# First q products of a decoder step: shift and scale in parts of 256, 256 and 512 features instead of two of 512, and cache loads issued right behind adaLN

## The chip, the cores and the metric

The kernel runs on one core of a Trainium2 chip. The metric is the device time of one execution in microseconds (us). Three executions of the kernel before the change took 1012.66, 1013.51 and 1015.45 us; the median is 1013.51 us. The profile shown below comes from one further execution, of 1013.97 us, whose records span 1012.2 us from the first to the last instruction.

## The reference

One layer of a decoder trunk for two groups of tokens that share the weights: a prompt of 512 tokens and 8 sample tokens, each sample token with 1024 cached tokens in pages of 128. The width is 1024, there are 16 heads of 64, and all data are float32.

```
m = adaLN(c) -> (shift1, scale1, gate1, shift2, scale2, gate2)   # silu(c) @ ada_w + ada_b
h = RMSNorm(x) * (1 + scale1) + shift1
z = h @ w_in  -> rg_x | rg_gate | q | k | v | forget logits | merge gate A | merge gate B
branch A: causal conv -> RG-LRU -> * gelu(rg_gate) -> @ w_proj_a
branch B: forgetting attention over q, k, v, log f -> @ w_proj_b
x = x + gate1 * ((sigmoid(gA) * A + sigmoid(gB) * B) @ w_o)
x = x + gate2 * SwiGLU(RMSNorm(x) * (1 + scale2) + shift2)
y = RMSNorm(x)
```

The sample tokens attend to cached keys and values, and to the running sum of a cached log forget value (`cache_logf`), all of which are gathered by a page table.

## The kernel before

**Tiling.** The activations lie transposed: eight tiles of 128 features by 520 tokens (512 prompt, 8 sample). Each matmul product takes 128 weight columns by half of the tokens (260), and is done with float32 values split in two parts: weights into `whi` and `wlo`, activations `h` into `hh` and `hl`. Each 128-feature step of a product is three matmuls (hi by hi, lo by hi, hi by lo). ACT casts the high part (`whi`, `hh`), DVE subtracts it for the low part (`wlo`, `hl`). A full product (128 output columns, all 8 feature tiles, both token halves) is 48 matmuls.

**The start.** SP issues, in this order, the parameters, the eight `x` tiles, the weights of adaLN for features 0 to 511 of shift1 and scale1 (`araw`, eight loads of 512 KB, one for each 128 rows of `ada_w`), a small constant load (`cs`: the identity), the first weights of q (`wraw`), and then adaLN's weights for features 512 to 1023. `first_mod` multiplies a loaded `araw` tile with silu(c): four matmuls of 256 columns side by side, written to four groups of 32 rows of one bank (`adaf`). `keep_busy` puts matmuls behind them whose results nobody reads (`idle`). `first_mod_end` copies the bank (`adas`, ACT), transposes it (`adaft`, PE), adds the biases (`mod`, DVE) and makes the amplitude (`n1amp`, DVE). Meanwhile ACT squares `x`, DVE adds the squares in two groups of four, PE sums them over the features with a matrix of ones (`ss`), and ACT and DVE take the root and the reciprocal over 128 by 520 (`r`). `norm_x` multiplies `x` by `r` (`xn`). `first_h(f)` makes `hh` and `hl` of one feature tile: ACT for the prompt tokens of `hh`, POOL for the eight sample columns of `hr` (two small operations), ACT for the cast of these eight, DVE for `hr` and `hl`.

**q.** Output columns are six tiles q0 to q5 here (q6 and q7 come later as ordinary products). q's products over features 0 to 511 run first (`qp` in the records: q0 to q2, then q3 to q5), with adaLN's second half between them, and are copied to `qpart`. Then q0 to q5 run over features 512 to 1023 (`q` in the records) and are added to `qpart` (`qadd`).

**What follows.** A numbered list of units (`chunks`, `units`) sets the order of the later products xr, gr, ga, gb, k, v and so on. A table (`KEYS`) says how many cached key pages are loaded with each unit, and DVE sums the pages in between (`key_sum`). Instructions are queued on each engine in a fixed order, and each engine works its queue in that order; `issue_after` fixes such an order between two instructions of different steps. A tile taken from a pool waits for the readers of the tile that had its buffer: `pg` has 7 buffers (adaLN's weights, key and value pages), `wraw` has 2 (product weights, and the cached log f `lfp`), `whi` and `wlo` have 3 each. A load that SP issues also waits until the load eight places ahead of it on SP has landed.

The cached log f (`past_load`) is one indirect load, issued by POOL once the page list `idx` has landed; `past_turn` transposes it (`lft`, PE) and sums it on POOL. In the kernel before, `past_load` comes with q4 and `past_turn` with q5, and the first key pages are loaded by POOL with q4.

## Time and profile before

| | |
|---|---|
| three executions | 1012.66, 1013.51, 1015.45 us |
| profiled execution | 1013.97 us, span of its records 1012.2 us |
| mean granted TensorE clock | 0.998 |
| PE busy | 990.4 us, 98% of the span |
| DVE, ACT, POOL busy | 791.0, 564.7, 342.8 us |
| DMA | 206.12 MB, mean 204 GB/s |
| first q product starts | 23.71 us |

PE is the engine that is busy nearly throughout. "Busy" counts the modelled length of an instruction; matmuls overlap, so the start of one to the start of the next is what a matmul takes of PE's time. In a timeline row stand the start, the time from the start of the first to the end of the last of the merged instructions, the engine, the line, the operation, what it writes and reads, the count, and in brackets how long the engine had been idle before and what released it. A float32 matmul that isn't split shows as two records (an `x8` row of `adaf` is four matmuls).

### The profile page before, as it was taken

How to read it: one execution, taken by the hardware profiler on the slowest of the kernel's cores; microseconds unless marked ns; L12 is line 12 of the kernel's file. 1: busy time of each engine (PE TensorE's matmuls, PEld its weight loads, DVE VectorE, ACT ScalarE, POOL GpSimd, SP SyncE). 2: the span in 40 equal slices, each digit the busy share in tenths (PEclk: the TensorE clock that was granted, in tenths of full speed). 3: DMA queues.
4: the chain of work that ended last, by engine and by line, in shares of the span. 5: the costliest groups of instructions: out<-in, count | busy, mean ns of one | idle time of the engine just before them, and what ended most of it. 6: DMA issues, size and time to landing. Idle time of an engine off the chain costs nothing.

```text
span 1012.2 us, 21376 instructions
## 1 busy us (share of the span) xinstructions
PE 990.4 (98%) x8020; PEld 913.6 (90%) x8020; DVE 791.0 (78%) x1400; ACT 564.7 (56%) x1161; POOL 342.8 (34%) x440
## 2 busy tenths in 40 slices
PE   5999999999999999999999999999999999999996
PEld 2899999999898988888888878999999999999996
DVE  5678899989999887887655454869888888779864
ACT  4524679866952477777783233554444444445453
POOL 1136121323243244654400001483342442434212
PEclk9999999999999999999999999999999999999999
DMA  9799856889879998997767995333334243233122
GB/s 335 262 315 288 242 170 190 264 261 298 277 234 354 326 308 267 321 276 239 254 204 264 332 337 161 85 94 96 97 92 126 63 126 97 71 106 105 63 64 85
DMA packets 164441, 206.12 MB, mean 204 GB/s; under 512 B 9826, under 2 KB 125170, under 8 KB 164274
## 3 DMA queue, kind: packets, MB, share of 16 engines
q1 hardware_dynamic: 147778, 152.19, 48.3%
q0 software_dynamic: 12880, 46.14, 13.9%
q10 hardware_dynamic: 3680, 6.42, 1.7%
q8 instruction: 63, 1.03, 0.4%
q14 instruction: 40, 0.33, 0.1%
HBM read 191.64 MB, written 13.09 MB: 202 GB/s over the span
## 4 chain that ended last, share of the span: by engine, by line
PE 88%; DMA 4%; ACT 4%; DVE 2%; issue 1%; SPq 0%; POOL 0%; ACTq 0%; DVEq 0%; POOLq 0%
PE fo L310 13%; PE wo L310 5%; PE gb L310 5%; PE ga L310 5%; PE xr L310 5%; PE pb L310 4%; PE k L310 4%; PE gr L310 3%; PE v L310 3%; PE pa L310 3%; PE pv L860 3%; DMA pg<-in_cache_v_dram 2%; PE qp L546 2%; PE q L546 2%; PE po L1327 2%; PE ada L377 2%
## 5 line engine op out<-in xcount | busy, mean ns | idle before, releaser
L249 ACT CAST whi<-wraw 128x1024 fp32r<-128x1024 f32 (+1 forms) x79 | 82.1, 1039 | 109.3 <-PE pb L310 34.5
L251 DVE TENSOR_TENSOR wlo<-wraw,whi 128x1024 fp32r<-128x1024 f32 (+1 forms) x79 | 98.7, 1250 | 21.8 <-ACT whi L249 19.0
L273 ACT CAST wb<-ws 128x512 fp32r<-128x512 f32 x72 | 44.8, 622 | 88.9 <-PE fo L310 61.9
L310 PE MATMUL fo<-ach,wb 128*128 128x260 f32 x512 | 93.4, 283 | 0.0
L274 DVE TENSOR_TENSOR wb<-wraw,wb 128x512 fp32r<-128x512 f32 x86 | 76.8, 893 | 5.1 <-ACT wb L273 4.4
L310 PEld LDWEIGHTS fo<-ach,wb 128*128 128x128 f32 x512 | 78.8, 188 | 0.0
L714 POOL DMA_DIRECT2D pg<-in_cache_k_dram x74 | 40.1, 542 | 107.2 <-DVE S L772 57.6
L264 POOL TENSOR_TENSOR ws<-wraw 128x512 f32<-128x512 f32 x18 | 23.7, 1317 | 153.8 <-DMA wraw<-in_w_fi_dram 104.7
L310 PE MATMUL fo<-acl,wb 128*128 128x260 f32 x256 | 72.2, 282 | 0.0
L273 ACT CAST wb<-wraw 128x512 fp32r<-128x512 f32 x86 | 53.6, 623 | 33.3 <-ACT cp L1725 6.2
L274 DVE TENSOR_TENSOR wb<-ws,wb 128x512 fp32r<-128x512 f32 x72 | 61.4, 853 | 13.0 <-ACT wb L273 11.3
L771 DVE TENSOR_TENSOR pg<-pg,qb 128x1024 f32<-128x1024 f32 x48 | 58.1, 1224 | 2.2 <-DMA pg<-in_cache_k_dram 2.2
L772 DVE TENSOR_REDUCE S<-pg 128x16 f32<-128x1024 f32 x48 | 57.3, 1206 | 0.2
L1284 POOL TENSOR_SCALAR p<-p,mu 128x128 f32<-128x128 f32 (+3 forms) x28 | 38.4, 1383 | 54.8 <-DVE mu L1280 35.0
L310 PEld LDWEIGHTS fo<-acl,wb 128*128 128x128 f32 x256 | 48.2, 188 | 0.0
L1278 ACT ACTIVATE p<-p,mu 128x128 f32<-128x128 f32 (+3 forms) x64 | 35.3, 553 | 18.2 <-DVE mu L1277 17.6
L310 PE MATMUL v<-hh,whi 128*128 128x260 f32 x128 | 37.3, 292 | 1.0 <-DVE S L828 0.5
L860 PE MATMUL pv<-pg,pw 128*32 128x512 f32 x256 | 37.1, 604 | 1.0 <-DMA pg<-in_cache_v_dram 0.9
L310 PE MATMUL k<-hh,whi 128*128 128x260 f32 x128 | 37.4, 292 | 0.0
L310 PE MATMUL gb<-hh,whi 128*128 128x260 f32 x128 | 37.3, 291 | 0.0
L310 PE MATMUL ga<-hh,whi 128*128 128x260 f32 x128 | 36.7, 286 | 0.5 <-ACT tA L1100 0.5
L310 PE MATMUL pb<-oh,whi 128*128 128x260 f32 x128 | 37.0, 289 | 0.2 <-ACT oh L1385 0.2
(1107 smaller groups left out, 3959.7 us busy)
## 6 DMA issues: line engine op xcount, KB each, us to landing
araw<-in_ada_w_dram SPq DMA_DIRECT2D x48, 512.0 KB, 7.9
wraw<-in_w_fi_dram SPq DMA_DIRECT2D x44, 512.0 KB, 4.5
pg<-in_cache_k_dram POOLq DMA_DIRECT2D x42, 512.0 KB, 5.7
pg<-in_cache_v_dram SPq DMA_DIRECT2D x42, 512.0 KB, 5.3
wraw<-in_w_in_dram SPq DMA_DIRECT2D x34, 512.0 KB, 6.9
wraw<-in_w_in_dram SPq DMA_DIRECT2D x11, 1024.0 KB, 8.2
pg<-in_cache_v_dram POOLq DMA_DIRECT2D x22, 512.0 KB, 6.5
pg<-in_cache_k_dram POOLq DMA_DIRECT2D x32, 256.0 KB, 5.1
```

The costliest lines, as they stand in the source:

```text
L249: state["act"] = act.copy(hi[:, :k1 - k0], src)
L251: state["last"] = dve.tensor_tensor(lo[:, :k1 - k0], src, hi[:, :k1 - k0].bitcast(F32), ALU.subtract)
L273: state["act"] = act.copy(t[:, :4], src)
L274: state["last"] = dve.tensor_tensor(t[:, 4:], src, t[:, :4].bitcast(F32), ALU.subtract)
L310: state["mm"] = pe.matmul(out[:, :t1 - t0], lhsT=wt[k], rhs=at, start=k == 0 and m == 0, stop=k == nk - 1 and m == 2)
L546: state["mm"] = pe.matmul(b[:, :HALF], lhsT=wt, rhs=at[:, t0:t1], start=k == 0 and m == 0, stop=k == 3 and m == 2)
L714: done.append(eng.dma_start(pg, cache[bass.ds(r, 1), :, c0:c1].rearrange("a p c -> (a p) c")))
L771: dve.tensor_tensor(pg, pg, q, ALU.mult)
L772: last = dve.tensor_reduce(S[r // 2][:, c:c + H], pg.rearrange("p (h d) -> p h d", d=DH), AX.X, ALU.add)
L860: pe.matmul(pv[0][32 * gq:32 * gq + 32, :], lhsT=pw[r][:, c:c + 32], rhs=pgs[gq // 2][:, 512 * hf:512 * hf + 512], start=j == 0, stop=j == ...
L1278: act.activation(p[:, :n + 128], p[:, :n + 128], AF.Exp, bias=mu[:, 0:1], scale=-1.0, accum_out=mu[:, 1:2])
L1284: (pool.tensor_scalar(p, p, mu[:, 2:3], None, ALU.mult) if a and i + 1 < KT else act.activation(p, p, AF.Copy, scale=mu[:, 2:3]))
```

## The change

**Parts.** adaLN's first shift and scale are made in three parts: features 0 to 255, 256 to 511 and 512 to 1023. A part of 256 takes four tiles of 512 KB; each tile holds two groups of 128 rows and comes by two loads of 256 KB (256 columns of shift, 256 of scale, 1 KB in a row). Its matmuls have 128 columns, four side by side, eight such groups in a part. The third part is loaded and multiplied as before. Of the `idle` matmuls between the tiles none are left; one stands behind x's second tile, one behind the fourth, and two behind the first part's transpose.

**The root.** The squares are added in one chain of eight. Five matmuls with one column each give the sums for 104 tokens at a time, the root and the reciprocal are taken over 104 by 5 values, five DVE operations spread them over diagonal matrices (`dg1`, with the identity, whose load is now issued ahead of adaLN's), and two matmuls with ones give `r1` on all rows, which ACT copies.

**q.** q0 to q2 run over features 0 and 1 (in tiles of 128) first, then q3 to q5 over 0 to 3, then q0 to q2 over 2 to 7, and then q3 to q5 over 4 to 7. The weights come as 256 rows by 384 columns.

**Loads.** The page list, the cached log f, q's last weights and the first ordinary chunk follow adaLN's last part directly. Two key pairs are loaded by SP ahead of q3. `past_turn` comes with q3, and one key sum more is placed ahead of the second half of q4.

The core of the diff:

```diff
+    sp.dma_start(cs[:, :C_ONE], cst[:, :C_ONE])
...
-    def first_mod(fh, acc, kqs):
+    def first_mod(part, acc, kqs):
+        if part < 2:
+            for kq in range(kqs[0], kqs[-1], 2):
+                raw = pgp.tile([128, 2, 512], F32, name="araw", tag="pg")
+                for v in range(2):
+                    c0 = 1024 * v + 256 * part
+                    sp.dma_start(raw[:, :, 256 * v:256 * v + 256],
+                                 ada_w[kq * 128:kq * 128 + 256, c0:c0 + 256].rearrange("(k p) c -> p k c", p=128))
+                for k in range(2):
+                    for g in range(4):
+                        m = pe.matmul(acc[32 * g:32 * g + 32, :128], lhsT=silc[:, kq + k],
+                                      rhs=raw[:, k, 128 * g:128 * g + 128],
+                                      start=kq + k == 0, stop=kq + k == KT - 1, tile_position=(0, 32 * g))
+            return
...
-            if fh == 0:
-                keep_busy(m, 1 if 2 < kq < KT - 1 else 0)
...
-    for j, (t0, t1) in enumerate(HALVES):
-        act.activation(r1[:, t0:t1], ssq[j][:, :HALF], AF.Sqrt, bias=eps, scale=1.0 / D)
-        dve.reciprocal(r1[:, t0:t1], r1[:, t0:t1])
...
+    for b in range(5):
+        pe.matmul(ps[:, b:b + 1], lhsT=sq[:, NB * b:NB * b + NB], rhs=ones[:, :1], start=True, stop=True)
+    rt = small("rt1", NB, 5, 1)
+    act.activation(rt, ps, AF.Sqrt, bias=eps[:NB], scale=1.0 / D)
+    dve.reciprocal(rt, rt)
+    dg = slot("dg1", NT, parts=NB)
+    for b in range(5):
+        dve.tensor_scalar(dg[:, NB * b:NB * b + NB], ident[:NB, :NB], rt[:, b:b + 1], None, ALU.mult)
+    first_mod(0, acc[0], range(0, 4))
+    r1 = slot("r1")
+    for j, (t0, t1) in enumerate(((0, 3 * NB), (3 * NB, NT))):
+        ps = bank(f"r1_{j}")[:, :t1 - t0]
+        pe.matmul(ps, lhsT=ones[:NB, :], rhs=dg[:, t0:t1], start=True, stop=True)
+        act.copy(r1[:, t0:t1], ps)
+    first_mod(0, acc[0], range(4, KT))
...
+    banks = [bank(f"qa{i}_{j}") for i in range(3) for j in range(2)]
+    q_step((0, 1), 0, 0, banks)
+    q_step((0, 1), 0, 1, banks)
+    first_mod(1, acc[1], range(0, 4))
...
+    banks = [bank(f"qb{i}_{j}") for i in range(3, 6) for j in range(2)]
+    q_step(range(4), 3, 0, banks, 0, 4)
+    first_mod(1, acc[1], range(4, KT))
...
+    banks = [bank(f"qc{i}_{j}") for i in range(3) for j in range(2)]
+    q_step(range(2, KT), 0, 2, banks)
+    first_mod(2, acc[2], range(4, 6))
...
+    sp.dma_start(prm, par)
+    sp.dma_start(ptb, pt.rearrange("a b -> (a b)")[None, :])
+    sp.dma_start(idx, pt.rearrange("a (b c) -> (a b) c", c=1))
+    for kp in (2, 3):
+        q_loads(kp, 3)
+        q_split(kp, qraw[kp, 3], 3, ends)
+    past_load()
     load_chunks(0)
...
+    first += [half_load(0, j, 0, sp) for j in (0, 2)]
...
+                if (i, j) == (4, 0):
+                    with tc.issue_after(state["mm"].ins):
+                        key_pages(2)
+                    with tc.issue_after(state["qadd"].ins):
+                        key_sum()
...
         if i == 3:
             split_upto(0)
             gate_load(0)
+            past_turn(0)
+            past_turn(1)
```

How the instructions stand on the engines is shown at three places. The first is PE from its first instruction to the first q product. Before (`ss` are the sums of squares, `adaf` adaLN's products):

```order
L564 MATMUL ss_0_114<-sq_118,cs 128x260
L564 MATMUL ss_1_115<-sq_118,cs 128x260
L484 MATMUL adaf_116<-araw,silc 32x256 x4
L564 MATMUL ss_0_114<-sq_137,cs 128x260
L564 MATMUL ss_1_115<-sq_137,cs 128x260
L484 MATMUL adaf_116<-araw,silc 32x256 x12
L493 MATMUL idle<-x,cs 128x260
L484 MATMUL adaf_116<-araw,silc 32x256 x4
```

Now (`r` are the two matmuls that spread the reciprocal root over all rows):

```order
L504 MATMUL idle<-x,cs 128x260 x2
L599 MATMUL ss_143<-cs,sq_118 104x1 x5
L489 MATMUL adaf_115<-araw,silc 32x128 x17
L610 MATMUL r_0_181<-dg_152,cs 128x312
L610 MATMUL r_1_184<-dg_152,cs 128x208
L489 MATMUL adaf_115<-araw,silc 32x128 x15
L513 MATMUL adaft_218<-cs,adas 128x128
L504 MATMUL idle<-x,cs 128x260 x2
L569 MATMUL qa_0_266<-hh,whi 128x260
```

The two `r` matmuls stand behind the first matmul of adaLN's third tile, and 15 matmuls of the first part stand behind them.

The second place is PE where the second part of adaLN ends, now between q3 to q5 over feature tile 0 (`qb`):

```order
L569 MATMUL qb_1_339<-hl,whi 128x260
L489 MATMUL adaf_116<-araw,silc 32x128 x3
L569 MATMUL qb_0_336<-hh,whi 128x260
L569 MATMUL qb_0_336<-hh,wlo 128x260
L569 MATMUL qb_0_336<-hl,whi 128x260
L513 MATMUL adaft_380<-cs,adas 128x128
L569 MATMUL qb_0_340<-hh,whi 128x260
```

All 32 matmuls of this part now stand behind the first q product, where before the first 512 features were done ahead of it.

The third place is POOL around the cached log f (`lfp`); `hr` are the sample columns of the feature tiles, two rows for each tile. Before:

```order
L903 COPY q_586<-qp 128x8 [waits DVE_49]
L438 DMA lfp<-in_cache_lf_dram,idx 64x2048 [waits DMAHW4_49,DMAHW7_49,DMAHW3_49,Activation_49]
L903 COPY q_586<-qp 128x8 [waits DVE_49]
```

Now, with the sample columns of tile 4 ahead and those of tiles 5, 6 and 7 behind:

```order
L533 TENSOR_TENSOR hr<-xn,n1amp 128x8 [waits DVE_49]
L534 TENSOR_TENSOR hr<-hr,mod 128x8 [waits Pool_49]
L439 DMA lfp<-in_cache_lf_dram,idx 64x2048 [waits DMAHW3_49,DMAHW2_49,Activation_49]
L533 TENSOR_TENSOR hr<-xn,n1amp 128x8
L534 TENSOR_TENSOR hr<-hr,mod 128x8 [waits Pool_49]
```

POOL issues `lfp` once `idx` has landed, and the sample columns of three feature tiles are queued behind it.

More of the change, by code (lines that the diff above doesn't have):

```diff
@@ L496, in first_mod_end, with keep_busy @@
+    def keep_busy(m, n, f=0):
+        for _ in range(n):
+            with tc.issue_after(m.ins) if m is not None else nullcontext():
+                m = pe.matmul(idle[:, :HALF], lhsT=ones, rhs=x[f][:, :HALF], start=True, stop=True)
+        return m
+    def first_mod_end(part, acc):
+        nb = 1 if part < 2 else 2
         sb = slot("adas", 256)
-        act.copy(sb, acc[:, :256])
-        tp = bank(f"adaft{fh}")
-        for b in range(2):
+        mods = act.copy(sb[:, :128 * nb], acc[:, :128 * nb])
+        tp = bank(f"adaft{part}")
+        for b in range(nb):
@@ L612, with q_step @@
[L612 to L616 removed]
+    def q_step(ks, g3, k, banks, n0=0, n1=6):
+        for n in range(n0, n1):
+            q_matmuls(ks, g3 + n // 2, n % 2, k, banks[n])
+    idle = bank("idle")
+    acc = [bank(f"adaf{part}") for part in range(3)]
+    m = None
+    for f in range(KT):
+        t = slot("sq1")
+        act.activation(t, x[f], AF.Square)
+        if f:
+            dve.tensor_tensor(sq, sq, t, ALU.add)
+        else:
+            sq = t
+        if f in (1, 3):
+            m = keep_busy(m, 1, f)
@@ L720, with half_load @@
     summed = [0] * 4
+    first = []
+    def half_load(s, j, half, eng=None):
+        pg = pgp.tile([128, 2, 512], F32, name="pg", tag="pg")
+        for a in range(2):
+            page_load(cache_k, s, j + a, pg[:, a], 512 * half, 512 * half + 512, eng)
+        return pg
     def key_halves(s, j, half):
```

210 lines of the change are left out of this document (106 added, 104 removed).

## The prediction

> **What bounds the kernel now.** I read the page's head first, then the windows by stage, the timelines of PE, ACT and DVE up to 60 us, the DMA rates in windows of 2 us, and last the waits. From the page, and from the windows (us; busy time of PE, PEld, DVE, ACT, POOL with counts; granted clock, DMA share, GB/s):
>
> ```profile
> span 1012.2 us, 21376 instructions
> 0.00:24.00 24.00, 13.91 (x89) 6.39 (x89) 11.43 (x17) 10.51 (x17) 1.89 (x14) 1.00 0.95 332
> 24.00:50.00 26.00, 25.66 (x222) 20.84 (x222) 16.39 (x28) 15.30 (x32) 5.87 (x15) 1.00 0.80 270
> 50.00:75.00 25.00, 25.00 (x213) 22.42 (x212) 20.00 (x57) 6.34 (x15) 9.91 (x21) 1.00 0.97 311
> 100.00:150.00 50.00, 50.00 (x405) 47.53 (x404) 45.92 (x61) 35.47 (x68) 10.20 (x19) 1.00 0.68 208
> ```
>
> PE idles for 10 us before 24 and hardly after. So there are two ways to gain: start the products earlier, or give PE less behind that start. The start, and PE's steps from there, from PE's timeline:
>
> ```profile
> 8.38 2.07 PE L564 MATMUL ss<-sq,cs 128*128 128x260 f32 x4 [8.38 <-DVE sq L559]
> 13.98 1.67 PE L484 MATMUL adaf<-araw,silc 128*32 128x256 f32 x24
> 15.58 0.71 PE L493 MATMUL idle<-x,cs 128*128 128x260 f32 x2
> 16.37 0.64 PE L484 MATMUL adaf<-araw,silc 128*32 128x256 f32 x8
> 20.48 0.64 PE L484 MATMUL adaf<-araw,silc 128*32 128x256 f32 x8
> 21.61 0.44 PE L500 MATMUL adaft<-cs,adas 128*128 128x128 f32 x2 [0.49 <-ACT adas L497]
> 23.71 0.39 PE L546 MATMUL qp<-hh,whi 128*128 128x260 f32 x1 [0.35 <-ACT whi L536]
> ...
> 29.72 0.64 PE L484 MATMUL adaf<-araw,silc 128*32 128x256 f32 x8
> 30.29 0.39 PE L546 MATMUL qp<-hh,whi 128*128 128x260 f32 x1
> 30.51 0.28 PE L546 MATMUL qp<-hh,wlo 128*128 128x260 f32 x1
> 30.63 0.28 PE L546 MATMUL qp<-hl,whi 128*128 128x260 f32 x1
> 31.55 0.64 PE L484 MATMUL adaf<-araw,silc 128*32 128x256 f32 x8
> ...
> 56.88 0.28 PE L546 MATMUL q<-hh,whi 128*128 128x260 f32 x1
> ...
> 546.87 1.07 PE L377 MATMUL ada<-araw,silc 128*32 128x512 f32 x8
> ```
>
> adaLN's tiles 4 to 7 run at 16.37 to 20.48: (20.48 - 16.37) / 3 = 1.37 us a tile, which is the DMA's pace. The first product, at 23.71, stands at the end of that stream. From there a matmul takes 0.12 us (30.51 to 30.63).
>
> **The start, step by step.** Rates of the DMA (windows, columns as above):
>
> ```profile
> 6.00:8.00 2.00, 0.00 (x0) 0.00 (x0) 1.34 (x3) 1.51 (x3) 0.00 (x0) 1.00 1.04 379
> 22.00:24.00 2.00, 1.65 (x8) 1.02 (x6) 1.28 (x5) 1.46 (x3) 1.18 (x6) 1.00 1.09 348
> 36.00:38.00 2.00, 2.00 (x19) 1.45 (x19) 0.00 (x0) 1.10 (x3) 0.00 (x0) 1.00 1.12 315
> 44.00:46.00 2.00, 2.00 (x19) 2.00 (x18) 1.69 (x3) 2.00 (x6) 1.27 (x4) 1.00 0.00 0
> ```
>
> Tile 0 has landed by 20.48 - 7 x 1.37 = 10.9, so `x` is through at 9.5, and at 9.7 with the constants now ahead. The first part is four tiles, 2.1 MB. Its rows of 1 KB are like those of q's weights, which run in the windows at 22 and 36: 348 and 315 GB/s. That makes 6.0 to 6.7 us; I take 6.3, so the part is there at 16.0 and its third tile at 14.4. If it kept the 379 GB/s of the 6 us window, it would be 15.2.
>
> The other chain is the root. Rows of ACT and DVE, for both chains:
>
> ```profile
> 21.18 0.37 ACT L497 COPY adas<-adaf 128x256 f32<-128x256 f32 x1 [6.62 <-PE adaf L484]
> 22.54 0.60 ACT L517 ACTIVATE hh<-xn,mod,n1amp 128x260 fp32r<-128x260 f32 x1 [0.99 <-DVE n1amp L510]
> 23.05 1.12 ACT L536 CAST whi<-wraw 128x512 fp32r<-128x512 f32 x2
> 34.99 0.73 ACT L604 COPY qp<-qp 128x260 f32<-128x260 f32 x2 [5.91 <-PE qp L546]
> ...
> 8.82 2.31 DVE L559 TENSOR_TENSOR sq<-sq,sq 128x520 f32<-128x520 f32 x3 [0.59 <-ACT sq L557]
> 13.75 3.41 DVE L572 RECIPROCAL r<-r 128x260 f32<-128x260 f32 x2 [2.62 <-ACT r L571]
> 17.20 2.53 DVE L576 TENSOR_TENSOR xn<-x,r 128x520 f32<-128x520 f32 x4
> 22.31 0.20 DVE L510 SCALAR_TENSOR_TENSOR n1amp<-mod,prm 128x36 f32<-128x36 f32 x1
> 157.52 0.22 DVE L820 TENSOR_SCALAR mk<-cs,st 32x32 f32<-32x32 f32 x1
> ```
>
> The squares are still summed at 8.82 + 2.31 = 11.1, since ACT's squares set that. Five one-column products are between nothing and five of the 0.52 us of an `ss` record, 2.6; the nearest rows are the two transposes in 0.44 us, so I take 1.3. Root, reciprocal and five small DVE operations are seven of about 0.22 (the row at 157.52), 1.5; with 0.5 for four hops between engines the diagonals stand at 14.4. The 3.41 us of the reciprocal are gone. The `r` matmuls have 520 columns together: 2.07 us by the `ss` row (two of 260), 2 x 0.71 = 1.4 by the later `idle` row; I take 1.4, to 15.8. ACT's last copy adds 0.4 and two `xn` 2 x 0.63: 17.5.
>
> adaLN's chain goes on when PE has finished its last 15 matmuls, which are held behind the `r` matmuls. Price of a group of four with 128 columns: 256 columns take 1.67 / 3 = 0.56 us each in a run; alone, 0.64 against 1.07 for 512. The difference of 0.43 for 256 columns, halved, taken from 0.56 gives 0.35. Bounds are 0.28 (half of 0.56) and 0.56. So 3.75 groups are 1.3, from 16.0 to 17.3; `xn` is done at 17.5, before DVE comes to `mod`.
>
> From there, before: `adaf` ends at 21.1, `n1amp` at 22.5, `hh` at 23.1, and then the weights' cast holds PE until 23.7. The cast now stands ahead of `hh`, under the transpose, so I take 1.4 + 0.6 + 0.1 = 2.1. The first product is at **19.4 instead of 23.71**: 4.3 us earlier.
>
> **What PE has behind the start.** Both kernels do the same 216 matmuls in the stretch that ends at 57.0 before (q0 to q5 over the first four feature tiles, q0 to q2 over the rest; the row at 56.88 is the 216th by count). Before: 216 x 0.12 = 25.9; eight groups of 256 at 0.57 (29.72 to 30.29), each with 0.2 for changing to adaLN and back (31.55 - 29.72 = 1.83, less nine products of 0.12 and the group), 6.2; transposes 0.4; total 32.5. It takes 57.0 - 23.7 = 33.3, so 0.8 is stall. Now: 25.9; the second part, which stood ahead of the products before, 8 x 0.35 = 2.8; the third part 8 x 0.57 = 4.6; six changes instead of eight 1.2; transposes 0.6; the same 0.8 of stall: 35.9. It ends at 19.4 + 35.9 = 55.3. The gain is **57.0 - 55.3 = 1.7 us**; the other 2.6 of the start go into adaLN's products, which now run in PE's full stretch.
>
> The stall may grow to about 2: each `h` waits for 1.4 us of amplitude work, for which 21 products (2.5 us) stand ready in part two and 18 (2.2 us) in part three. Splits move, but none is added, and the copies of q's banks stay on ACT, 59% busy there.
>
> **The loads.** Before, the DMA stands still from 44 to 46 (0 GB/s), so two key pairs and the log f there (1.5 MB) displace nothing. The price at nothing rests on that hole; without it they would cost q's last weights 1.5 MB / 348 = 4.3 us. What POOL has behind `lfp`:
>
> ```profile
> idx<-in_pt_dram SPq DMA_DIRECT2D x1, 0.2 KB, 7.8
> araw<-in_ada_w_dram SPq DMA_DIRECT2D x16, 512.0 KB, 9.2
> ...
> 53.45 1.04 POOL L438 DMA_INDIRECT lfp<-in_cache_lf_dram,idx  x1 [0.81 <-issue]
> ```
>
> On SP, `idx` stands behind a q load that needs the buffer of the third part's third tile. PE reads that tile after 108 products, the second part, two tiles and four changes: 13.0 + 2.8 + 1.1 + 0.8 + 0.6 for the tile's own, so at 37.7; with four issues of 0.5 `idx` goes out at 39.7 and lands, after 7.8 us, at 47.5. `lfp` takes 1.04, the columns of tile 5 0.5, ACT's cast 0.2, `hl` 0.7: 49.9. PE comes to that `hl` after 174 products, at 19.4 + 20.9 + 2.8 + 4.6 + 1.2 + 0.6 + 0.8 = 50.3. So it costs nothing, with a cover of 0.4; beyond it, every us that `idx` lands later is a us.
>
> **The rest.** After 57 both do the same work. PE stays full (50.00 of 50 at 100), and DVE, at 45.92 of 50, still waits there for others:
>
> ```profile
> DVE wlo L251 <- ACT whi L249: 4.4, 4, 2.0
> ```
>
> DVE therefore follows a PE that is 1.7 us ahead. Sum: 1013.97 - 1.7 = 1012.3 for the profiled execution. The median lies 0.46 below it, so **1011.9 us** is predicted.
>
> **Rivals.**
>
> *Cheaper parts.* With the part at 15.2 and groups at 0.28, PE's last 15 matmuls end at 15.8 + 1.0 = 16.8 (the `r` matmuls hold them), 0.5 earlier; the second part takes 2.2, 0.6 less; and there is no stall, 0.8. 1011.9 - 1.9 = 1010.0. For it: the next tile is there when PE returns. Against: the 1 KB windows.
>
> *Fewer waits at the values.* PEld waits for value pages later on; earlier key sums could take that away:
>
> ```profile
> PEld pv L860 <- DMA pg<-in_cache_v_dram: 3.6, 4, 1.6
> ```
>
> 1011.9 - 3.6 = 1008.3. Against it: `KEYS` paces the pages by PE's units as before, and only one pair is summed earlier.
>
> *The array starts slow.* The `ss` row takes 0.52 us a record and the `idle` row 0.36 for the same shape, later; up to 13.98 PE needed 5.6 us of work for the full rate. Now that work begins at 11.1, and the `idle` matmuls between tiles are gone. If PE were still slow for 5.6 us after the first product, half of it, 2.8, would be lost: 1014.7. Against it: the remaining matmuls fill 11 to 17 nearly, and slow ones fill it more. [...]
>
> *The root is the bound.* With 2.6 for the one-column products and 2.1 for `r`, as by the `ss` row, adaLN's last matmuls are held 2.0 longer: 1013.9.
>
> *POOL is held by `idx`.* The one on the other side. It is slower than before once `idx` takes over 7.8 + 0.4 + 1.7 = 9.9 us to land. At 11.8, the longest landing of an adaLN tile, and with SP held once more for its longest wait on PE (2.3), both in these rows:
>
> ```profile
> DMA to landing us min/median/max: 5.7/9.2/11.8
> SPq L481 <- PE adaf L484: 5.8, 5, 2.3
> ```
>
> it is 4.0 + 2.3 - 0.4 = 5.9 later: 1017.8. For it: three tiles' sample columns stand behind one load. Against: far less data is queued ahead of `idx` than before.
>
> **How the numbers follow.** Forecast 0.41, between 1010.9 and 1013.4; cheaper parts 0.14; values 0.10; slow array 0.15; root 0.08; POOL 0.12. Three executions spread over 2.8 us, and 0.3% (3 us) is about what can be told from no change. Faster by that, under 1010.5: the second and third, 0.24. Slower, over 1016.5: POOL, 0.12. Within: 0.64. The range of 1009.0 to 1015.5 takes in the parts' and the array's bounds and leaves out POOL's far end and the values.
>
> **What would show it.** The first `qa` product at 19.4 (18.9 to 21); `r` matmuls ending ahead of adaLN's fourth tile; `adaf` x8 rows of 128 columns at 0.7 us a tile; the first q2 sum on DVE some 1.7 us earlier than before; `lfp` on POOL beginning between the sample columns of tiles 4 and 5 without a wait over 2 us; DMA moving at 44 to 46. I am wrong if PE shows waits of over 2 us between 20 and 55, if the `qa` matmuls stand 0.24 us apart, or if PE's waits after 85 us differ from before's.

## The result and the profile after

Six executions of the changed kernel took 1007.15 to 1008.85 us, median 1007.99; six of the kernel before, beside them, 1012.66 to 1015.45, median 1013.62. The ratio is 0.9943, with a 95% interval from 0.993 to 0.9956: 5.6 us faster, where 1.6 were forecast and the range ended at 1009.0. The profiled execution took 1008.59 us with a span of 1006.9, 5.3 us less than the one shown of before.

PE's timeline after, from the sums of squares to the first q product, one row of each part of adaLN's matmuls between the q products, and the last of the 216 q matmuls (`qc`); `r` is spread at L610:

```profile
11.84 1.89 PE L599 MATMUL ss<-cs,sq 128*104 128x1 f32 x10 [3.44 <-DVE sq L591]
13.66 2.34 PE L489 MATMUL adaf<-araw,silc 128*32 128x128 f32 x34
15.93 2.10 PE L610 MATMUL r<-dg,cs 104*128 104x312 f32 x4
17.97 1.92 PE L489 MATMUL adaf<-araw,silc 128*32 128x128 f32 x30
21.71 0.39 PE L569 MATMUL qa<-hh,whi 128*128 128x260 f32 x1 [0.24 <-ACT hh L532]
...
26.68 1.08 PE L489 MATMUL adaf<-araw,silc 128*32 128x128 f32 x32
27.69 0.39 PE L569 MATMUL qb<-hh,whi 128*128 128x260 f32 x1
...
36.31 1.07 PE L497 MATMUL adaf<-araw,silc 128*32 128x256 f32 x16
37.31 0.39 PE L569 MATMUL qb<-hh,whi 128*128 128x260 f32 x1
...
56.13 0.28 PE L569 MATMUL qc<-hl,whi 128*128 128x260 f32 x1
```

The first product came at 21.71, not at 19.4: `r` took 2.10 us and the 30 records behind it 1.92, while 32 such records take 1.08 a few us later. The array was slow up to about 20 us. The granted clock doesn't show it: it reads 1.00 here (the number ahead of the DMA's share in this window of after), so the rate at the start has to be read from the length of the rows.

```profile
14.00:16.00 2.00, 2.00 (x35) 1.48 (x27) 1.20 (x6) 0.04 (x1) 0.00 (x0) 1.00 1.08 359
```

The stretch behind it was shorter than forecast: it ends at 56.13 + 0.12 = 56.25. Before, it ends later than the prediction says, whose count was five matmuls short: the 216th is the last one of q2, ahead of the first of q3, and a `qt` transpose stands between them. It ends at 57.6 (PE's timeline of before):

```profile
57.49 0.28 PE L546 MATMUL q<-hl,whi 128*128 128x260 f32 x1
57.61 0.27 PE L907 MATMUL qt<-cs,qp 128*8 128x128 f32 x1
```

So 57.6 - 56.25 = 1.4 us are gained here. To see where the other 3.9 come from, I cut both programs at the first matmul of four products and at the last of the FFN (the SwiGLU, from the first `fi` to the last `fo`). PE's timeline, before:

```profile
84.97 0.37 PE L310 MATMUL xr<-hh,whi 128*128 128x260 f32 x1
...
291.73 0.28 PE L310 MATMUL pa<-gh,whi 128*128 128x260 f32 x1
...
532.57 0.37 PE L310 MATMUL pb<-oh,whi 128*128 128x260 f32 x1
...
645.69 0.28 PE L310 MATMUL fi<-h2h,whi 128*128 128x260 f32 x1
...
1002.11 0.28 PE L310 MATMUL fo<-acl,whs 128*128 128x240 f32 x1
```

And after:

```profile
83.62 0.36 PE L311 MATMUL xr<-hh,whi 128*128 128x260 f32 x1
...
290.21 0.28 PE L311 MATMUL pa<-gh,whi 128*128 128x260 f32 x1
...
528.26 0.37 PE L311 MATMUL pb<-oh,whi 128*128 128x260 f32 x1
...
641.53 0.28 PE L311 MATMUL fi<-h2h,whi 128*128 128x260 f32 x1
...
996.72 0.28 PE L311 MATMUL fo<-acl,whs 128*128 128x240 f32 x1
```

The lead is 1.35 us at `xr`, 1.52 at `pa`, 4.31 at `pb`, 4.16 at `fi` and 5.39 at the end of `fo`. The stretch from `pa` to `pb` holds the value pages, and gave 2.8. The FFN, `fi` to `fo`, which the change doesn't touch and where PE shows no wait and PEld one of 0.3 us in either profile, took 356.42 us before and 355.19 after: 1.2 us.

The wait of PEld (PE's loading of weights) for value pages (groups of waits: total, times, longest) was 3.6 us in 4 before; after:

```profile
PEld pv L937 <- DMA pg<-in_cache_v_dram: 1.2, 2, 1.0
```

### The profile page after: what moved, and what is told of

Same layout as the page of the kernel before. It is cut to its first block, busy times and chain, and to the rows that moved or that the text cites. A ratio compares the mean times of both kernels' runs of the same rounds, so it can differ in the third digit from the quotient of the medians.

```text
span 1006.9 us, 21535 instructions
## 1 busy us (share of the span) xinstructions
PE 986.5 (98%) x8084; PEld 916.1 (91%) x8084; DVE 789.2 (78%) x1410; ACT 566.8 (56%) x1165; POOL 342.6 (34%) x436
## 4 chain that ended last, share of the span: by engine, by line
PE 87%; ACT 5%; DVE 4%; issue 2%; DMA 1%; POOL 0%; SPq 0%; DVEq 0%; POOLq 0%; ACTq 0%
PE fo L311 13%; PE wo L311 5%; PE pb L311 4%; PE gb L311 4%; PE k L311 4%; PE ga L311 4%; PE v L311 4%; PE xr L311 3%; PE pa L311 3%; PE pv L937 3%; PE gr L311 2%; PE po L1410 2%; PE ada L378 2%; PE ptt L1376 2%; PE fi L311 1%
## 5 line engine op out<-in xcount | busy, mean ns | idle before, releaser
L250 ACT CAST whi<-wraw 128x1024 fp32r<-128x1024 f32 (+1 forms) x79 | 82.2, 1041 | 96.1 <-PE pb L311 34.5
L275 DVE TENSOR_TENSOR wb<-wraw,wb 128x512 fp32r<-128x512 f32 x86 | 73.1, 850 | 4.8 <-ACT wb L274 4.2
L785 POOL DMA_DIRECT2D pg<-in_cache_k_dram x70 | 37.9, 542 | 99.3 <-DVE S L849 57.5
L311 PE MATMUL pa<-gh,wlo 128*128 128x260 f32 x128 | 36.3, 284 | 0.8 <-DVE wlo L252 0.8
```

What stands on the lines that cost most here:

```text
L250: state["act"] = act.copy(hi[:, :k1 - k0], src)
L275: state["last"] = dve.tensor_tensor(t[:, 4:], src, t[:, :4].bitcast(F32), ALU.subtract)
L311: state["mm"] = pe.matmul(out[:, :t1 - t0], lhsT=wt[k], rhs=at, start=k == 0 and m == 0, stop=k == nk - 1 and m == 2)
L785: done.append(eng.dma_start(pg, cache[bass.ds(r, 1), :, c0:c1].rearrange("a p c -> (a p) c")))
```

## The experiments

Times are medians. "Before" was run beside each group: 1012.61, 1012.67, 1012.82 and 1012.31 us. Three questions are asked: whether the waits for value pages went because of the change, what the start and the loads are each worth, and what made the FFN faster. The edits are shown shortened: `...` stands for lines left out, and remarks behind `#` are added here.

**The kernel before, once more.** No edit.

> The kernel before, unchanged, profiled a second time, to see which of its waits come back. After the change PE stands 1.4 us ahead at 290 us and 5.4 ahead at the end; the steps between lie at 311 (1.0), 376 (1.2) and 422 us (0.9), where PE waits for value pages before, and in a slow drift of 1.2 from 700 us on. If these waits belong to the order of the loads, this profile shows them at the same places (PEld for value pages 3.6 us in 4, give or take 0.5), and its matmuls in fi and fo keep the pace of the first profile. If they are chance of one execution, the sum of the waits differs by over 1.5 us or the drift is gone.

It took 1010.87 us with a span of 1009.1. PE's timeline of this second profile:

```profile
85.80 0.37 PE L310 MATMUL xr<-hh,whi 128*128 128x260 f32 x1
...
292.60 0.28 PE L310 MATMUL pa<-gh,whi 128*128 128x260 f32 x1
...
529.53 0.37 PE L310 MATMUL pb<-oh,whi 128*128 128x260 f32 x1
...
642.65 0.28 PE L310 MATMUL fi<-h2h,whi 128*128 128x260 f32 x1
...
999.04 0.28 PE L310 MATMUL fo<-acl,whs 128*128 128x240 f32 x1
```

From `pa` to `pb` it needs 236.93 us, not 240.84, and among its waits there is none of `pv` for a value page. The waits that the changed kernel seemed to have lost are chance of one execution, and the first profile was one of the long ones. The FFN takes 356.39 again: that difference is no chance.

**A later start.**

```diff
-            keep_busy(m, 2)
+            keep_busy(m, 5)
```

> The changed kernel with five idle matmuls instead of two ahead of the first q product, so that PE starts 3 x 0.52 - 0.24 = 1.3 us later and the rest is unchanged: its lead over the kernel before at 110 to 290 us is undone (1.4 to 0.1). Theory 'phase' (the waits for value pages went because PE and SP reach them 1.4 us earlier): they come back, 1012 to 1013.5 us. Theory 'loads' (they went because two key pairs and one key sum are done earlier): 1008.0 + 1.3 = 1009.3 us, with PEld waits for value pages near 1.2 us. Theory 'start is slack' (nothing of the start counts): 1008.0 us.

1007.42 us (ratio to before 0.9942, 0.9929 to 0.9954). The waits did not come back, but PE wasn't later either: it came to `pa` at 289.24, against 290.21 in the changed kernel. So the run tests neither "phase" nor "start is slack"; what speaks against "phase" is the second profile of before. The edit stands behind these two rows of PE's timeline, and they are already shorter than in the changed kernel (2.10 and 1.92):

```profile
15.97 1.53 PE L610 MATMUL r<-dg,cs 104*128 104x312 f32 x4
17.43 1.07 PE L489 MATMUL adaf<-araw,silc 128*32 128x128 f32 x30
```

The array came to full rate during `r`, some 3 us earlier than in the changed kernel's profile (about 17 us against 20, an estimate from these rows), and that gave back what the three idle matmuls took: the first product stood at 21.04.

**The changed kernel, once more.** No edit.

> The changed kernel, unchanged, profiled again. FFN 355.2 us as in its first profile, if the pace belongs to the build. If the start is a matter of when the array is granted its full rate, the 30 adaLN records behind r take either 1.9 or 1.1 us, and q's first product comes at 21.7 or 20.3. The stretch from pa to ptt (62.85 us at first, 62.0 and 63.76 in two profiles of the kernel before) moves by over 0.5 us, if the waits for value pages are chance.

1007.37 us (0.9949, 0.9936 to 0.9962). PE's timeline:

```profile
16.12 1.95 PE L610 MATMUL r<-dg,cs 104*128 104x312 f32 x4
18.01 1.07 PE L489 MATMUL adaf<-araw,silc 128*32 128x128 f32 x30
...
20.91 0.39 PE L569 MATMUL qa<-hh,whi 128*128 128x260 f32 x1 [0.24 <-ACT hh L532]
```

The same program, and the 30 records take 1.07: the moment of full rate is a matter of the execution. `pa` to `pb` took 238.28 us (238.05 at first), the FFN 355.13.

Four profiles side by side, in us. The executions differ in when `x` arrives, so the start is counted from the end of ACT's last square.

| | before | before, again | after | after, again |
|---|---|---|---|---|
| end of the last square | 10.15 | 10.81 | 10.45 | 10.76 |
| from there to the first q product | 13.56 | 13.74 | 11.26 | 10.15 |
| from there to `xr` | 74.82 | 74.99 | 73.17 | 72.00 |
| `xr` to `pa` | 206.76 | 206.80 | 206.59 | 206.58 |
| `pa` to `pb` (value pages) | 240.84 | 236.93 | 238.05 | 238.28 |
| `pb` to `fi` | 113.12 | 113.12 | 113.27 | 113.23 |
| `fi` to the last of `fo` | 356.42 | 356.39 | 355.19 | 355.13 |
| from there to the end of the span | 10.07 | 10.07 | 10.22 | 9.72 |

**The array kept busy.** The first try:

```diff
-        if f in (1, 3):
+        if 0 < f < 7:
             m = keep_busy(m, 1, f)
```

> The changed kernel with an idle matmul behind each of x's tiles 1 to 6 instead of two of them, so that PE works without a pause from 5.5 us on. In the changed kernel's profile the two r matmuls take 2.10 us and the 30 records behind them 1.92; with the late start the same took 1.53 and 1.07. Theory 'slow array' (PE runs at half rate until it has been busy long enough, in some executions until 16.8, in others until 19.8 us): full rate is there by 14 us, the first q product comes at 20.0 to 20.5 instead of 21.7, and the time is 1006.7 us. Theory 'landing' (adaLN's tiles set the start): the first product stays at 21.5 or so, 1008.0 us.

1005.46 us (0.993, 0.9917 to 0.9943), with the first product at 19.54 (9.0 after the last square). More was gained than expected, though the rate came and went. PE's timeline, and a window (columns as in the prediction; the granted clock is the number ahead of the DMA's share):

```profile
11.76 1.08 PE L599 MATMUL ss<-cs,sq 128*104 128x1 f32 x10 [1.23 <-DVE sq L591]
...
14.52 2.10 PE L610 MATMUL r<-dg,cs 104*128 104x312 f32 x4
```

```profile
14.00:16.00 2.00, 2.00 (x9) 1.25 (x5) 0.41 (x3) 0.04 (x1) 0.00 (x0) 0.50 1.09 360
```

PE was fast at 11.76 (1.08 us for `ss`, which takes 1.89 in the changed kernel), had paused for 1.23 us ahead of it, and was at half clock at 14 to 16. The second try closes that pause and keeps `r` ahead of the third tile:

```diff
-        if f in (1, 3):
-            m = keep_busy(m, 1, f)
+        if f:
+            m = keep_busy(m, 1 if f < 7 else 2, f)
...
-    first_mod(0, acc[0], range(4, KT))
+    first_mod(0, acc[0], range(4, KT), rm)   # its matmuls behind the r matmuls
```

> The changed kernel with idle matmuls behind x's tiles 1 to 6 (one each) and 7 (two), and the r matmuls ahead of adaLN's third tile. With one idle matmul a tile to tile 6 the granted clock was 1.00 at 10 to 12 us, 0.50 at 14 to 16 and 0.81 at 16 to 18: PE had paused for 1.23 us ahead of the one-column products, and r took 2.10 us again. Theory 'a pause of over a microsecond costs the rate for 3.4 us': without this pause the clock stays at 1.00 from 10 us on, r takes 1.05 us, the 4th tile (in the old-root run PE waits for it until 16.1) then sets the end of adaLN, the first q product comes at 18.5 us and the time is 1004.5 us. Theory 'the rate falls for other reasons' (a window of its own): 0.50 shows again between 10 and 20 us, and the time stays at 1005.5 us.

PE's timeline:

```profile
12.15 1.07 PE L600 MATMUL ss<-cs,sq 128*104 128x1 f32 x10
13.15 1.08 PE L490 MATMUL adaf<-araw,silc 128*32 128x128 f32 x32
14.48 1.14 PE L611 MATMUL r<-dg,cs 104*128 104x312 f32 x4 [0.25 <-DVE dg L606]
...
18.94 0.39 PE L570 MATMUL qa<-hh,whi 128*128 128x260 f32 x1 [0.30 <-ACT hh L533]
```

Without the pause the rate stays (the granted clock reads 1.00 in every window from 8 to 20 us), and `r` takes 1.14 us, as the theory of the pause has it. The time is 1005.69 us (0.9929, 0.9916 to 0.9942): no different from the first try, and 1.2 us above what I expected. The first product is 8.1 us after the last square, 0.9 earlier than in the first try, but `xr` only 0.2 (70.7 and 70.9). They beat the changed kernel (1007.37 us, run beside the first try) by 1.9 and 1.7 us in the medians (one execution of the first try took 1008.46); these are the better versions here.

**The root as before**, in the changed kernel: squares in two groups, four `ss` matmuls of 260 columns, root and reciprocal over 128 by 520.

```diff
-    pe.matmul(ps[:, b:b + 1], lhsT=sq[:, NB * b:NB * b + NB], rhs=ones[:, :1], start=True, stop=True)
...
+    pe.matmul(ssq[j][:, :HALF], lhsT=ones, rhs=sq[:, t0:t1], start=f == 3, stop=f == KT - 1)
...
+    act.activation(r1[:, t0:t1], ssq[j][:, :HALF], AF.Sqrt, bias=eps, scale=1.0 / D)
+    dve.reciprocal(r1[:, t0:t1], r1[:, t0:t1])
```

> The changed kernel with the root as before: squares added in two groups of four, four matmuls of 260 columns, root and reciprocal over 128 by 520. Theory 'root costs' (in the slow array r stands behind 1.9 us of one-column products and takes 2.1 itself, and 15 adaLN matmuls wait behind it): the first xn at 17.2 instead of 18.4 us, first q product at 20.3 to 20.8, time 1006.8 us. Theory 'root brings the start' (DVE's 3.41 us of reciprocals hold xn and mod): first q product at 22 or later, 1008.5 us or more.

PE's timeline:

```profile
19.76 0.59 PE L569 MATMUL qa<-hh,whi 128*128 128x260 f32 x1 [1.45 <-ACT hh L532]
20.14 0.42 PE L569 MATMUL qa<-hh,wlo 128*128 128x260 f32 x1
```

The first product came earlier, at 19.76, as "root costs" says, and yet the time is 1008.03 us (1005.23 to 1009.13; 0.9951, 0.9937 to 0.9964), as in the changed kernel. Behind DVE's long reciprocals PE waited for 1.45 us, and the products then took 0.42 us instead of 0.28 and stood 0.22 apart instead of 0.12, for 3.4 us: half rate, with a granted clock of 0.50 at 20 to 22. `xr` stands 72.19 us after the last square, between the changed kernel's 73.17 and 72.00, and 0.7 us of the time belong to the FFN (355.89 instead of 355.2; see the last experiments). By this run the new root is worth about nothing in time.

**The start without the loads.** The changed kernel with its log f, first key pairs and early key sum as before:

```diff
-    past_load()              # behind adaLN
...
-    first += [half_load(0, j, 0, sp) for j in (0, 2)]
...
-                if (i, j) == (4, 0):
-                    with tc.issue_after(state["mm"].ins):
-                        key_pages(2)
-                    with tc.issue_after(state["qadd"].ins):
-                        key_sum()
...
-            past_turn(0)     # with q3
-            past_turn(1)
...
+                past_load()  # with q4
...
+            key_pages(2)
...
+            past_turn(0)     # with q5
+            past_turn(1)
```

> The changed kernel with its cached log f, its first key pages, its turn of the log f and its number of early key sums placed as in the kernel before; parts, root and q's order stay. After q's first 216 matmuls PE is 0.75 us ahead of the kernel before. Theory 'phase': the lead at 290 us is 0.75 or so, the waits for value pages may go in part: 1009 to 1011 us. Theory 'loads': the waits come back whole: 1013.6 - 0.75 = 1012.9 us.

1012.34 us (0.9992, 0.9982 to 1.0002): nothing is left of the gain, and the waits for value pages have no part in it (`pa` to `pb` 236.85). It is lost at `ga`. PE's timeline and windows:

```profile
95.99 0.28 PE L311 MATMUL ga<-hh,whi 128*128 128x260 f32 x1
98.67 0.58 PE L311 MATMUL ga<-hh,wlo 128*128 128x260 f32 x1 [2.40 <-DVE wlo L252]
```

```profile
95.00:98.00 3.00, 1.27 (x11) 1.06 (x9) 3.00 (x4) 3.00 (x10) 1.70 (x5) 1.00 1.05 406
98.00:101.00 3.00, 2.33 (x11) 2.33 (x11) 3.00 (x5) 1.04 (x2) 1.62 (x4) 0.56 0.91 334
```

PE waits 2.40 us for DVE, and then runs at half clock (0.42 us a product, 0.56 granted at 98 to 101): together 4.0 us. Another 0.7 us lie in the FFN (355.88).

**The loads without the start.** The kernel before with the two key pairs by SP, and one key sum ahead of the second half of q4.

```diff
+    first += [half_load(0, j, 0, sp) for j in (0, 2)]
...
+                if (i, j) == (4, 0):
+                    with tc.issue_after(state["mm"].ins):
+                        key_pages(2)
+                    with tc.issue_after(state["qadd"].ins):
+                        key_sum()
```

> The kernel before with only the two key pairs issued by SP ahead of q and one key sum ahead of the second half of q4; parts, root, q's order and the cached log f as before. Theory 'phase': PE's lead at 290 us is at most the 0.65 us that PE wins between 57 and 110 in the changed kernel, 1013.0 us or more. Theory 'loads': the waits for value pages go as in the changed kernel, 1009.5 to 1010.5 us.

1012.99 us (0.9999, 0.9991 to 1.0008): alone they bring nothing, as the prediction has it.

**One of the two alone.** In the changed kernel, only the log f late, then only the key pairs and the sum late:

```diff
-    past_load()              # behind adaLN
...
-            past_turn(0)     # with q3
-            past_turn(1)
...
+                past_load()  # with q4
...
+            past_turn(0)     # with q5
+            past_turn(1)
```

```diff
-    first += [half_load(0, j, 0, sp) for j in (0, 2)]
...
-                if (i, j) == (4, 0):
-                    with tc.issue_after(state["mm"].ins):
-                        key_pages(2)
-                    with tc.issue_after(state["qadd"].ins):
-                        key_sum()
...
+            key_pages(2)     # with q4
```

> The changed kernel with the cached log f issued and turned where the kernel before does it; key pairs by SP and the early key sum stay. With all three undone PE waited 2.4 us at ga for DVE's wlo and then ran at half rate for 3.4 us, and the stretch from xr to gate took 27.3 instead of 23.25 us. Theory 'early sum' (one key sum, two DVE operations of 1.2 us, falls into that stretch otherwise): no wait here, 1007.7 us. Theory 'log f': the wait is back, 1011.7 us.

> The changed kernel with the first two key pairs issued by POOL in q4 and without the early key sum, as in the kernel before; the cached log f stays early. Theory 'early sum': the wait at ga is back (2 us or more, and the half rate behind it), xr to gate 27 us, 1011.7 us. Theory 'log f': no wait, 1007.7 us.

Neither theory had it: both cost. With the log f late it is 1010.88 us (0.9975, 0.9965 to 0.9985), with the sum late 1013.08 (1.0001, 0.999 to 1.0011). About 1 us of either is the FFN's (356.25 and 356.28 instead of 355.2); the rest lies between `xr` and `pa` (210.82 and 210.47 instead of 206.6). With the log f late, SP's queue and PE (groups of waits), and ACT's timeline:

```profile
SPq L214 <- PE lft L451: 1.1, 1, 1.1
```

```profile
PE ga L311 <- ACT whi L250: 1.3, 1, 1.3
PE ga L311 <- DVE wlo L252: 0.9, 1, 0.9
```

```profile
98.98 0.26 ACT L744 ACTIVATE fe<-fa 128x65 f32<-128x65 f32 x1 [11.00 <-DMA fa<-fld]
...
100.73 1.03 ACT L250 CAST whi<-wraw 128x1024 fp32r<-128x1024 f32 x1
```

The late log f holds one of the two `wraw` buffers until `lft`, so a product's weights that SP issues at 61.6 in the changed kernel go out at 70.2 here, and ACT waits 6.52 us for weights at 80. That alone isn't what `ga` pays for: before, ACT waits 6.27 us at 74 and PE doesn't pause at `ga`. What holds `ga` here is ACT's next long wait, 11.00 us for the forget logits (`fa`), whose load takes 11.2 us to land (3.0 and 4.4 in the two profiles of the changed kernel); the cast of `ga`'s weights stands behind it, and PE pauses twice. Why `fa` lands so late isn't shown, nor whether it does so in every execution; the nine took 1009.05 to 1012.15 us. With the sum late, DVE's timeline:

```profile
88.82 2.35 DVE L844 TENSOR_TENSOR pg<-pg,qb 128x1024 f32<-128x1024 f32 x2
...
95.62 2.34 DVE L845 TENSOR_REDUCE S<-pg 128x16 f32<-128x1024 f32 x2
97.87 1.21 DVE L252 TENSOR_TENSOR wlo<-wraw,whi 128x1024 fp32r<-128x1024 f32 x1
```

Four key sums (a product and a reduction each) stand in a row ahead of the `wlo` that `ga` needs; in the changed kernel DVE is through with them by 91.0. PE waits 1.5 us at `xr` and 1.9 at `ga`.

**What makes the FFN faster.** First, its instructions moved in PE's program, in the kernel before:

```diff
-            keep_busy(m, 3)
+            keep_busy(m, 4)
```

> The kernel before with four idle matmuls instead of three behind adaLN's first transposes, where PE waits for the weights' cast anyway (it may cost 0.2 us). Nothing of the FFN changes but the place of its instructions in PE's program. From the first matmul of fi to the last of fo the kernel before takes 356.42 and 356.39 us in two profiles, the changed one 355.19, the changed one with a late start 355.36. Theory 'place' (the pace of the matmuls belongs to the build): it moves by 0.2 to 1.5 us here too. Theory 'state' (buffers or loads that the change left behind speed the FFN): it stays at 356.4, and the time at 1012.6 us.

The FFN took 356.37 us, the time 1013.05 (1.0001, 0.9992 to 1.001): it doesn't matter where the instructions stand. Then all buffers in SBUF moved together:

```diff
+    pad = keep.tile([128, 16], F32, name="pad")
+    pool.memset(pad, 0.0)
     cs = keep.tile([128, NCONST], F32, name="cs")
```

> The kernel before with 64 unused bytes reserved in front of its buffers, so that every operand of its matmuls in SBUF lies 64 bytes further; no instruction of PE, ACT or DVE is changed (POOL clears the 64 bytes once). In builds whose matmul operands lie at the same addresses the FFN took the same time (before 356.42 and 356.39, with one idle matmul more 356.37; changed 355.19, again 355.26, warm array 355.12), in builds whose operands lie elsewhere another (355.36, 355.88, 355.89, 356.27). Theory 'addresses': it moves off 356.4 by 0.2 us or more here. Theory 'program': it stays within 0.1 of 356.4.

356.39, as in before, and 1012.36 us (1.0003, 0.9992 to 1.0014): my theory of addresses fell in this form. (The changed kernel's second profile took 355.13, not the 355.26 of this expectation.) What was left is how the tiles lie relative to each other. The activations' buffers are used in turn; one more taken at the start turns them all by one, while weights and PSUM banks stay. Or the same 64 bytes stand between the activations' and the weights' buffers:

```diff
+    pool.memset(slot("spare"), 0.0)            # buffers turned
     cs = keep.tile([128, NCONST], F32, name="cs")
```

```diff
     heap = ctx.enter_context(tc.tile_pool(name="heap", bufs=60))
+    padp = ctx.enter_context(tc.tile_pool(name="padp", bufs=1))   # one tile of 64 bytes
     wp = ctx.enter_context(tc.tile_pool(name="wp", bufs=3))
```

> The kernel before, with one activation buffer used up at the start (POOL clears it once, nobody reads it), so that every later tile of the activations lies one buffer further in the round; weights, banks and instruction orders are unchanged. Theory 'placement' (the matmuls' pace depends on how the tiles lie relative to each other): fi to fo leaves 356.4 us by 0.2 or more, within 355.1 to 356.5, the span of all builds so far. Theory 'something else in the build': 356.4, within 0.1.

> The kernel before, with 64 unused bytes between the activations' buffers and the weights' buffers: weights, pages and small tiles move 64 bytes, activations stay; instruction orders are unchanged. Theory 'placement': fi to fo leaves 356.4 by 0.2 us or more. If it stays within 0.1, 64 bytes between weights and activations don't matter, and it is the activations' round alone or nothing of the kind.

> The changed kernel with one activation buffer used up at the start, as in the kernel before with its buffers turned. Theory 'placement': fi to fo leaves 355.2 us, most likely upwards (355.4 to 356.4), and the time is 0.2 to 1.2 us above the changed kernel's 1007.4 to 1008.0. Theory 'something else': 355.2, and 1007.4 to 1008.0 us.

The kernel before, turned, and the changed kernel, turned (PE's timelines, first of `fi` and last of `fo`):

```profile
643.95 0.29 PE L311 MATMUL fi<-h2h,whi 128*128 128x260 f32 x1
...
999.75 0.27 PE L311 MATMUL fo<-acl,whs 128*128 128x240 f32 x1
```

```profile
641.47 0.28 PE L312 MATMUL fi<-h2h,whi 128*128 128x260 f32 x1
...
997.43 0.28 PE L312 MATMUL fo<-acl,whs 128*128 128x240 f32 x1
```

355.80 us instead of 356.4, and 355.96 instead of 355.2. With the weights moved against the activations it is 355.88. Placement holds: turned on both sides, the FFN no longer favours the changed kernel (355.80 and 355.96). In time: the changed kernel turned takes 1008.56 us (0.996, 0.9945 to 0.9975); the kernel before, turned and with its weights moved, 1011.59 and 1011.19 us, one execution each. Turned against turned, the change is thus worth about 3.0 us, as far as a single execution of before can tell.

**The better version, turned.** The second try above with the same extra buffer.

> The version with the array warm and kept so (1005.69 us), with one activation buffer used up at the start. The start should be as there: the clock at 1.00 from 11 us on, first q product at 8.1 us after x's last square, or 18.9 us. Theory 'placement': the time differs from 1005.7 by what fi to fo differs from 355.1, up to 1.3 us. Otherwise 1005.7 us.

1006.35 us (0.9945, 0.9931 to 0.9958), FFN 355.92. The first product is again 8.1 us after the last square. The start's gain holds; the 0.7 us above 1005.69 are about what the FFN lost.

## Why the prediction was wrong

**The base.** The sum was made against one execution of before that had long waits for value pages. From `pa` to `pb` it took 240.84 us; three more profiles with the same buffers took 236.93, 238.93 and 238.67. The three executions shown had a median of 1013.51, while those beside the experiments had 1012.3 to 1012.8. About 1 us of the miss is this.

**"After 57 both do the same work."** This step failed; the sum put everything behind 57 at nothing. The work is the same, but not its time: with other buffers the same matmuls ran 1.2 us faster in the FFN, and the stretch from `xr` to `pa` was 0.2 shorter. That a gain of placement came with this change is an accident of it: with both kernels turned, the FFN is 0.2 us longer in the changed one.

**The start.** The size came out near, by errors that cancel. The first product was forecast 4.3 us earlier; counted from the last square it was 2.3 to 3.6 earlier (two profiles of before against two of after). The terms that failed: `r` at 1.4 (2.10 and 1.95), the one-column products at 1.3 (1.89), and the 15 matmuls from 16.0 to 17.3, which ran from 17.97 to 19.9 (18.01 to 19.1 in the second profile). All three were priced by rows of a fast array, in a place where it is still slow. The 0.5 for four hops between engines is an estimate that no run shows: ACT's root begins 0.04 us behind `ss`, DVE's reciprocal 0.03 behind the root, and `dg` 0.04 behind the reciprocal (rows at 13.77, 14.07 and 14.30 of ACT and DVE, after). The stretch behind was forecast at 35.9 and took 34.5: adaLN's groups with their changes at 8.6 took 6.2, counted to the start of the next product (the rows at 26.68 and 36.31 show four groups of 128 columns in 1.01 us and two of 256 in 1.00, changes included, against 0.35 and 0.57 each without them), and the stalls took about 1 more than the 0.8 of the sum. At `xr` the gain is 1.6 to 3.0, 2.3 on average, against the 1.7 forecast. Its own end of 57.0 for before was 0.6 too early.

**The loads at nothing.** The price holds in the kernel before (1012.99 us) and not in the changed one, where leaving the loads late costs. I read the 4.4 us in which DVE waits for ACT's casts as slack, and concluded that DVE follows a PE that is ahead. In the new order one key sum more that is left for later makes the low weights of `ga` late on DVE, and a late log f goes with a late cast of `ga`'s weights on ACT: the one kernel is 5 us slower, the other 3, about 1 us of each being placement in the FFN. The loads bring no time of their own; they keep the start's gain.

**`idx` and POOL.** `lfp` was forecast at 47.5 and went out at 47.71, but that is luck. `idx` went out at 41.7, not at 39.7, and landed in 3.1 us, not in 7.8, so the page list was there at 44.8; what set `lfp` were the sample columns of tile 4, which POOL began at 46.45, and 0.7 us of waiting behind them for something other than `idx`. That it costs nothing was right: it stands between the columns of tiles 4 and 5, as forecast, and PE shows no wait for it. The DMA moves at 44 to 46 (windows of after):

```profile
44.00:46.00 2.00, 2.00 (x29) 1.39 (x22) 0.06 (x1) 0.37 (x1) 0.00 (x0) 1.00 0.91 242
```

**The signs I named.** The first product lay outside 18.9 to 21 in the first profile and inside in the second (20.91). adaLN's groups ran at about 1.0 us a tile while the array was slow and at 0.5 later, not at 0.7. The `r` matmuls ended at 18.0 with adaLN's 15 matmuls still behind them. The first q2 sum on DVE came later than before, not earlier, since it now queues behind the last splits and some small operations; PE didn't wait for it. The `qa` matmuls were not 0.24 apart, nor did PE wait over 2 us between 20 and 55. PE's waits after 85 did differ from before's, and so they do between two executions of the kernel before.

**The rivals.** "Fewer waits at the values" has the time (1008.3) and not the mechanism: the second profile of before has none of these waits, and the loads alone leave 1.8 us of them, so they go and come by themselves. "The array starts slow" and "the root is the bound" had the right cause in the wrong place: the rate was missing ahead of the first product, where it cost about 2 us, and not behind it. The half by which the first of them prices the slow rate fits two rows of PE's timeline of before: two groups of 256 columns take 1.01 us to the start of the next row at 10.96, and 0.57 at 16.37. "Cheaper parts" was right in a price, 0.25 a group in a run against its 0.28, but the 15 matmuls ahead of the first product were dearer, and the stalls grew. "POOL is held by `idx`" didn't come.

**The account.** From the means of before's four profiles with the same buffers (one of them with one idle matmul more) and of the changed kernel's two: 2.5 from the last square to `xr`, 1.2 in the FFN, 0.2 from `xr` to `pa`, 0.7 from `pa` to `pb`, 0.2 at the end, less 0.1 from `pb` to `fi`: 4.7 of the 5.3 us between the medians of 1012.67 and 1007.37. The 0.7 is less than these stretches scatter between executions, and the last 0.6 isn't explained.

## What to carry to other kernels

Profile the kernel before twice: a wait that is there in only one of two profiles is no term of a sum, neither as a gain to come nor as a base. Ahead of the first dense matmuls, price PE's work by rows from the same stretch, and fill the pauses there with idle matmuls: it brought 1.9 us for four more short matmuls. A change of 0.6% moved buffers about here, and the FFN, which it doesn't touch, took 1.2 us less; turn them once, on both sides, before a fraction of a per cent is put down to its idea.

## What the runs showed of the hardware

Some pauses of PE of 1.23 to 2.40 us were followed by half rate, and others of 1.5 and 1.9 us were not. After a pause of 1.23 us (the array kept busy, first try) the granted clock read 0.50 at 14 to 16 and 0.81 at 16 to 18; without it (second try) 1.00 from 8 to 20. After 1.45 us (old root) it read 0.95 at 18 to 20, 0.50 at 20 to 22 and 0.70 at 22 to 24; after 2.40 (the start without the loads) 0.56 at 98 to 101 and 0.87 at 101 to 104; after 1.25 with 0.87 a little later (log f late) 0.84 at 100 to 105 and 0.82 at 105 to 110. Taken as shares of time at 0.50, with the rest at 1.00, each of the last three comes to 3.4 us of half clock, an estimate from these windows. After the pauses of 1.5 and 1.9 us (sum late) it read 1.00 at 84 to 88, 88 to 92, 96 to 100 and 100 to 104. What decides between the two isn't shown.

The moment of full rate moves between executions of the same program: the 30 records took 1.92 us from 17.97 in one and 1.07 from 18.01 in the next, so full rate came about 2 us earlier in the second profile, an estimate from these rows.

At the start the granted clock doesn't show the slow rate: it reads 1.00 at 14 to 16 us in the changed kernel, where 34 records took 2.34 us against 1.08 for 32 later. The fall in the first try it does show, with 0.50 at 14 to 16.

The FFN's time went with how its tiles lie in SBUF relative to each other. In the kernel before it took 356.4 us, 356.39 with all buffers moved by 64 bytes together, 355.80 with the activations' buffers turned, and 355.88 with the weights moved by 64 bytes against the activations. Its 2950 or so matmuls took 356.37 to 356.42 us in all four profiles with before's placement (one of them shifted as a whole by 64 bytes), 355.12 to 355.19 in all four with the changed kernel's, and 355.36 to 356.28 in ten profiles of other placements. Why a placement is fast isn't shown, nor whether the PSUM banks, which also differ between the two kernels, have a share in their difference. Nor does any run show whether the 0.35% (1.2 of 356.4 us) is a wait at all.
